# Attention on one Trainium2 core: the norm of the queries by products in four 32-column tiles beside the products with v, turned once, and one out-projection moved to the last tile

## The chip, the cores and the metric

The kernel runs on one core of a Trainium2 chip. The metric is the time on the device, in microseconds, of one execution of the whole program. The time before is the median of three runs; a separate execution was recorded by the hardware profiler, and every number on a stage or an instruction comes from that one.

## The reference

The program is a network of four layers on a sequence of 1024 tokens with 16 meta tokens ahead of them (1040 columns in the kernel, 9 blocks: one of 16 and eight of 128). Layers 0 and 3 are sliding-window attention, layer 1 an mLSTM, layer 2 an HGRN2. The change touches the attention layers alone.

```python
def rmsnorm(x, g):
    xf = x.astype(jnp.float32)
    y = xf * lax.rsqrt(jnp.mean(xf * xf, axis=-1, keepdims=True) + EPS)
    return (y * g.astype(jnp.float32)).astype(x.dtype)

def sliding_window_attention(q, k, v, sinks, valid):
    ...
    s = jnp.einsum('bnqhgd,bnkhd->bnhgqk', qb, kk) * (A_HD ** -0.5)
    ...
    s = jnp.where(mask[None, :, None, None], s, -jnp.inf)
    sink = sinks.astype(jnp.float32).reshape(A_KV, g, 1)
    m = jnp.maximum(s.max(axis=-1), sink)
    e = jnp.exp(s - m[..., None])
    p = e / (e.sum(axis=-1) + jnp.exp(sink - m))[..., None]
    o = jnp.einsum('bnhgqk,bnkhd->bnqhgd', p, vv)
    return o.reshape(bsz, lp, A_W)

def attention_branch(u, w_in, q_gain, k_gain, sinks, w_out, valid, pos):
    bsz, lp, _ = u.shape
    q, k, v, z = _split(u @ w_in, (A_W, A_KVW, A_KVW, A_W))
    q = rope(rmsnorm(q.reshape(bsz, lp, A_HEADS, A_HD), q_gain), pos)
    k = rope(rmsnorm(k.reshape(bsz, lp, A_KV, A_HD), k_gain), pos)
    v = v.reshape(bsz, lp, A_KV, A_HD)
    o = sliding_window_attention(q, k, v, sinks, valid)
    return (o * jax.nn.silu(z.astype(jnp.float32))).astype(u.dtype) @ w_out
```

There are 16 query heads and 4 key heads of 64 columns. The norm of q is one number for each token and head: the mean of 64 squares, to the power -1/2.

## The kernel before

**Layout.** Activations lie transposed: features on the 128 partitions, tokens along the free axis. The tokens are cut into three chunks, `CHUNKS`, of 400, 384 and 256 columns, with blocks (0, 1, 2, 3), (4, 5, 6) and (7, 8). In the last attention layer (layer 3) the 16 meta tokens are not needed as queries, so its chunks (`LAST_CHUNKS`) hold three, three and two blocks. One attention layer has eight tiles t = 0..7, each of 128 features: two query heads, hh = 0 and 1.

**Products.** Matmuls of a projection (`proj`, L255) run in a rounded type, as three products for high and low halves of weights and activations; weights come by DMA, and `split` (L188 on ScalarE, L189 on VectorE) makes the halves. Matmuls in plain f32 (the norm, the products with v) appear in the trace as two records each.

**Queries.** `qk_proj` projects one tile of q, chunk by chunk. `evac` (L520, L521) writes the scaled q and its squares, `sq`, into temporaries of the pool `t` (five buffers, three for each chunk), and issues four DMAs on SP that rotate q for rope. `finish` hangs three steps behind a chunk, at delays `D_Q` of 2000, 4000 and 6000 ns of planned work: the norm, rope, and `q_split`. For q the norm is `columns`: for each block one matmul with the squares of 128 tokens as weights and two columns of a mask as the moving operand (L535), which gives one column per head and a row per token; ScalarE takes the logarithm (L537) and two exponentials (L539) into the small tile `rs` (four buffers), and in chunk 0 GpSimd negates four of them (L541). `stat` (L546) is the norm of the keys and is not touched.

**Softmax.** `mixers` cuts a tile into pairs of units (blocks 0; 1; 2 and 3; 4 and 5; 6; 7 and 8, both heads). `S_step` makes the scores (L615, L616) and the softmax, which reads `rs`: copy (L635), select (L636), maximum (L637, L638), exponential (L640), reciprocal (L642) and scaling (L644). `T_step` turns the probabilities on TensorE (L661) and masks them into `Pt` (L664). `V_step` multiplies with v (L683), each head in 64 columns of the array, and on a unit marked last copies the result to the row `R["o", t]` (L686). In the list of steps V_step of pair k - 2 comes first, then for each head T_step of pair k - 1 and S_step of pair k.

**Order.** The order of TensorE is written out by hand, as a list of steps `[cost, function, prefetch]`; the other engines are put in order by the framework's scheduler, with the softmax steps at a higher priority. `weave` mixes the softmax steps of a tile with its fill, in proportion to planned cost. `chain` strings the fill together from `parts` and inserts the hanging steps at their due times; what is due after the end hangs over to the next tile (`hang`). The fill of tile t is the q projection of t + 1, the gate projection `zc[t - 1]` (from t = 1 on), in t = 0 of layer 3 the v projection, in t = 3 the second tile of keys, and an out-projection (`proj_out`, L338, with adds into x, L341) in t = 2 (`oc[1]`) and t = 4 (`oc[3]`). `oc[5]` and `oc[7]` follow after the layer. The splits of an out-projection's operand, `splits`, are put 2500 ns (`Y_AHEAD`) ahead of its products. The last loop of `layer_a` moves a `q_split` that would come too early behind the last scores of the tile before. The final loop of the program runs the list and issues each prefetch 12 us of planned work ahead.

**Buffers.** [...] The rows of o, k, cos and sin share nine buffers of the pool `r`.

Of the kernel before, what the change touches and what calls it, by code (L numbers as in the profile page):

```python
# [11 lines left out]
AF = mybir.ActivationFunctionType  # L12
ALU = mybir.AluOpType
PSUM = bass.MemoryType.PSUM

P = 128
# [13 lines left out]
def blk(b):  # L30
    return (0, NMETA) if b == 0 else (NMETA + P * (b - 1), P)
# [9 lines left out]
ROWS, TMPS, RAWS, YS, QS = 9, 5, 2, 3, 6  # L41
XS = 14
GAP, BURST = 200.0, 1300.0
KT_LAG = 500.0
NORM_AT = (4000.0, 0.7), (5000.0, 0.5), (8000.0, 0.5)
Y_LAST, Y_EARLY, Y_AHEAD = 3, 8, 2500.0
# [5 lines left out]
MM = 1.0 / 2.4  # L52
# [58 lines left out]
def hybrid_kernel(ctx: ExitStack, tc: tile.TileContext, ins, out, layers=(0, 1, 2, 3)):  # L111
# [38 lines left out]
    def psa():  # L150
        return psum("pa", 1)
# [289 lines left out]
    def layer_a(i, j, first, last, fin):  # L441
# [13 lines left out]
            sp.dma_start(R["cos"], ins["rope"][0])  # L455
            sp.dma_start(R["sin"], ins["rope"][1])

        order = {}

        def k_split(j):  # L460

# [53 lines left out]
        def qk_proj(src, gcol, work, fsplit, ch, scales=None):  # L515
            late = {}

            def evac(acc, n, c0, cn):
                late[n] = dst, sq, rot = work(n, c0, cn)
                s.activation(dst, acc[:, :cn], AF.Identity, scale=R["cons"][:, gcol : gcol + 1])  # L520
                s.activation(sq, acc[:, :cn], AF.Square)  # L521
                for q in range(4):
                    o = q ^ 1
                    sp.dma_start(rot[32 * q : 32 * q + 32], dst[32 * o : 32 * o + 32])

            def finish(n, c0, cn):
                cs = slice(c0, c0 + cn)

                def columns():
                    sq = late[n][1]  # L530
                    st, qcols = psa(), [blk(b)[0] - c0 for b in CHUNK_BLOCKS[n] if blk(b)[0] >= c0]
                    w = 2 * len(qcols)
                    R["rs", scales, n] = rs = small(24).rearrange("p (z b) -> p z b", z=3)
                    for k, z in enumerate(qcols):
                        pe.matmul(st[:, 2 * k : 2 * k + 2], sq[:, z : z + P], R["masks"][:, 0:P:64],  # L535
                                  start=True, stop=True)
                    s.activation(rs[:, 2, :w], st[:, :w], AF.Ln, bias=eps, scale=1.0 / 64)  # L537
                    for z, power in ((0, -0.5), (1, 0.5)):
                        s.activation(rs[:, z, :w], rs[:, 2, :w], AF.Exp, scale=power)  # L539
                    if n == 0:  # L540
                        g.tensor_scalar(rs[:, 2, :4], rs[:, 0, :4], -1.0, None, op0=ALU.mult)  # L541

                def stat():
                    dst, sq, rot = late[n]
                    st = psa()
                    pe.matmul(st[:, :cn], R["masks"][:, 0:P], sq, start=True, stop=True)  # L546
                    rstd_from(st, sq, cn, 64)

                def rope():
                    dst, sq, rot = late[n]  # L550
                    v.tensor_tensor(dst, dst, R["cos"][:, cs], op=ALU.mult)
                    v.tensor_tensor(rot, rot, R["sin"][:, cs], op=ALU.mult)
                    v.tensor_tensor(dst, dst, rot, op=ALU.add)
                    if scales is None:
                        v.tensor_tensor(dst, dst, sq, op=ALU.mult)

                first = [4 * cn * MM, stat, None] if scales is None else [110 * len(CHUNK_BLOCKS[n]), columns, None]
                return [(D_Q[0], first), (D_Q[1], [0.0, rope, None]),
                        (D_Q[2], fsplit(lambda: late[n][0], n, c0, cn))]

            return proj(src, evac, ch), [finish(n, *c) for n, c in enumerate(ch)]

# [36 lines left out]
        def mixers():  # L599
# [97 lines left out]
            for k in range(len(pairs) + 2):  # L697
                seg = pairs[k][0]["t"] if k < len(pairs) else 8
                v2, t1, s0 = (pairs[j] if 0 <= j < len(pairs) else None for j in (k - 2, k - 1, k))
                if v2:  # L700
                    put(seg, 470, V_step, v2, len(v2[0]["unit"]))
                for hh in range(2):
                    if t1:
                        put(seg, 110, T_step, t1[hh], len(t1[hh]["unit"]))
                    if s0:
                        step = put(seg, 236, S_step, s0[hh], len(s0[hh]["unit"]))
                        if s0[hh]["last"]:
                            order["S", s0[hh]["t"], s0[hh]["n"]] = step
            return segs

        zc = {t: gate_proj(win[12 + t], lambda t=t: R["o", t], chunks) for t in range(8)}
# [24 lines left out]
        for t in range(8):  # L736
# [7 lines left out]
            if t in (2, 4):  # L744
                z, (q, fin) = zc[t - 1], qg[t + 1]
                parts += [(flat(z[:2]), []), tile_of(q[:1], fin[:1]), (z[2], []), tile_of(q[1:], fin[1:])]
                splits, products = outs(oc[t - 1])
                parts.append((products, [(-Y_AHEAD, z) for z in splits]))
            elif t < 7:
                parts.append(tile_of(*qg[t + 1]))  # L750
            if t % 2 or t == 6:
                parts.append((flat(zc[t - 1]), []))
            fill, hang = chain(parts)
# [2 lines left out]
        for t in range(1, 8):  # L756
            for n in range(3):
# [2 lines left out]
                k = at.index(id(order["S", t - 1, n]))  # L760
                if q < k:
                    body.insert(k, body.pop(q))
        return head, body, oc[5], oc[7]

    def layer_b(i, j, fin):
# [708 lines left out]
```

## Time and profile before

| | us |
|---|---|
| median of three runs | 2649.59 |
| lowest and highest run | 2643.7 and 2650.41 |
| the profiled execution | 2639.39 |
| its span, first to last instruction | 2637.2 |
| mean granted TensorE clock in it | 0.997 |

The page of a profile gives for each engine its busy time; PE is TensorE's matmuls and PEld its weight loads, which run beside them. A row of a group of instructions names the line, the engine, the operation and the tiles (out<-in), then the shapes, the count, the busy time and the mean duration of one in ns, the idle time of the engine ahead of them and what ended it. A row of the timeline has the start and the length in us and the count of merged instructions. A row of busy times by stretch has the stretch, its length, then for PE, PEld, DVE, ACT and POOL the busy time and the count, the granted clock, the DMA share and GB/s.

In layer 0 the products with v (L683) lie between 77 and 435 us of the span, in layer 3 between 2236 and 2583 us; the two layers between are not touched.

### The profile page before, as it was taken

Reading aid. Unit: us, or ns where it says so; the run is one execution under the profiler, and the core shown is the slowest. Engines: PE = TensorE matmul, PEld = TensorE weight load, DVE = VectorE, ACT = ScalarE, POOL = GpSimd, SP = SyncE. Lnnn points to the kernel's source line nnn. Section 1 sums busy time; section 2 is a strip of 40 time slices with the busy share of each in tenths; the row PEclk is TensorE's granted clock in tenths of the full one; section 3 lists DMA queues with packets and bytes.
Section 4 is the critical chain, followed back from the end, with each engine's and each line's share of the span. In section 5 each row is a group of like instructions: output and inputs, shape, how many; then the busy total and the mean of one; then the engine's idle time right before and its main releaser. Section 6 shows DMA issues by size and latency. Waiting matters only on the chain.

```text
span 2637.2 us, 54958 instructions
## 1 busy us (share of the span) xinstructions
PE 2578.4 (98%) x20848; PEld 2460.5 (93%) x20848; DVE 1880.7 (71%) x5127; ACT 1672.0 (63%) x4525; POOL 147.9 (6%) x465
## 2 busy tenths in 40 slices
PE   7999999999999999999999999999999999999999
PEld 6899988899999999999999999999999999999989
DVE  6777777974747474647464678979787979677776
ACT  7768686565454545454544657878585867768683
POOL 1000000000000000000000000111001001000000
PEclk9999999999999999999999999999999999999999
DMA  4211111021111111111111101011110111111102
GB/s 139 60 36 49 52 38 39 25 66 57 41 49 43 55 41 57 41 57 41 57 41 49 48 27 50 26 38 34 38 38 30 42 62 45 53 45 52 50 25 88
DMA packets 74040, 126.80 MB, mean 48 GB/s; under 512 B 11552, under 2 KB 25760, under 8 KB 73776
## 3 DMA queue, kind: packets, MB, share of 16 engines
q1 hardware_dynamic: 73776, 123.29, 15.0%
q8 instruction: 164, 2.69, 0.4%
q14 instruction: 100, 0.82, 0.1%
HBM read 108.40 MB, written 4.26 MB: 43 GB/s over the span
## 4 chain that ended last, share of the span: by engine, by line
PE 77%; DVE 12%; ACT 7%; issue 2%; DMA 2%; SPq 0%; POOL 0%; DVEq 0%; ACTq 0%; POOLq 0%
PE pj L255 36%; PE pj L338 16%; PE pj L300 10%; PE po L683 2%; PE po L898 1%; PE pa L912 1%; PE pt L661 1%; DVE t L408 1%; PE po L900 1%; PE pm L615 1%; DVE ul L189 1%; PE pm L616 1%; PE pa L535 1%; ACT Sm L640 1%; DVE X L1117 1%
## 5 line engine op out<-in xcount | busy, mean ns | idle before, releaser
L255 PE MATMUL pj<-uh,wh 128*128 128x384 f32 (+2 forms) x2592 | 889.2, 343 | 3.1 <-ACT uh L188 3.1
L255 PE MATMUL pj<-ul,wh 128*128 128x384 f32 (+2 forms) x2592 | 834.4, 322 | 2.9 <-DVE ul L189 2.7
L255 PE MATMUL pj<-uh,wl 128*128 128x384 f32 (+2 forms) x2592 | 832.2, 321 | 0.1
L255 PEld LDWEIGHTS pj<-uh,wh 128*128 128x128 f32 x2592 | 490.5, 189 | 32.1 <-issue 17.0
L255 PEld LDWEIGHTS pj<-ul,wh 128*128 128x128 f32 x2592 | 490.5, 189 | 12.6 <-DVE ul L189 5.5
L255 PEld LDWEIGHTS pj<-uh,wl 128*128 128x128 f32 x2592 | 490.1, 189 | 0.5 <-DVE wl L189 0.4
L189 DVE TENSOR_TENSOR wl<-wr,wh 128x512 fp32r<-128x512 f32 x336 | 228.5, 687 | 55.4 <-ACT wh L188 52.1
L300 PE MATMUL pj<-wh,uh 128*128 128x256 f32 x896 | 267.6, 299 | 0.0
L341 DVE TENSOR_TENSOR x<-x,pj 128x384 f32<-128x384 f32 (+2 forms) x480 | 234.8, 509 | 40.4 <-PE pj L338 38.6
L188 ACT CAST wh<-wr 128x512 fp32r<-128x512 f32 x337 | 202.8, 615 | 90.7 <-PE pj L338 28.4
L338 PE MATMUL pj<-yh,wh 128*128 128x384 f32 (+2 forms) x768 | 252.2, 328 | 0.0
L300 PE MATMUL pj<-wh,ul 128*128 128x256 f32 x896 | 251.9, 281 | 0.0
L300 PE MATMUL pj<-wl,uh 128*128 128x256 f32 x896 | 251.8, 281 | 0.0
L338 PE MATMUL pj<-yl,wh 128*128 128x384 f32 (+2 forms) x768 | 247.4, 322 | 3.1 <-DVE yl L189 3.1
L338 PE MATMUL pj<-yh,wl 128*128 128x384 f32 (+2 forms) x768 | 247.0, 322 | 0.0
L300 PEld LDWEIGHTS pj<-wh,uh 128*128 128x128 f32 x896 | 168.7, 188 | 2.6 <-issue 0.3
L300 PEld LDWEIGHTS pj<-wl,uh 128*128 128x128 f32 x896 | 168.8, 188 | 2.0
L300 PEld LDWEIGHTS pj<-wh,ul 128*128 128x128 f32 x896 | 168.8, 188 | 0.0
L428 DVE SCALAR_TENSOR_TENSOR t<-pj,t 128x384 f32<-128x384 f32 (+2 forms) x192 | 98.6, 514 | 98.1 <-ACT t L427 97.7
L429 ACT ACTIVATE t<-t 128x384 f32<-128x384 f32 (+2 forms) x240 | 117.7, 490 | 77.8 <-DVE t L428 76.7
L188 ACT CAST yh<-r 128x384 fp32r<-128x384 f32 (+2 forms) x120 | 57.4, 478 | 154.4 <-PE pj L338 139.9
L338 PEld LDWEIGHTS pj<-yl,wh 128*128 128x128 f32 x768 | 144.9, 189 | 5.0 <-DVE yl L189 4.7
(236 smaller groups left out, 5129.0 us busy)
## 6 DMA issues: line engine op xcount, KB each, us to landing
wr<-in_b_win SPq DMA_DIRECT2D x128, 256.0 KB, 2.8
wr<-in_a_win SPq DMA_DIRECT2D x80, 256.0 KB, 2.7
wr<-in_c_win SPq DMA_DIRECT2D x64, 256.0 KB, 2.7
r<-rowsd SPq DMA_DIRECT2D x16, 520.0 KB, 5.4
wr<-in_a_wout SPq DMA_DIRECT2D x32, 256.0 KB, 2.8
wr<-in_b_wout SPq DMA_DIRECT2D x32, 256.0 KB, 2.7
t<-t SPq DMA_DIRECT2D x96, 48.0 KB, 2.0
wr<-in_c_wout SPq DMA_DIRECT2D x16, 256.0 KB, 2.7
```

The source lines that it names most:

```text
L188: s.copy(h, src)
L189: v.tensor_tensor(l, src, h.bitcast(F32), op=ALU.subtract)
L255: pe.matmul(acc[:, :cn], a[:, k, :], b[:, k, c0 : c0 + cn], start=(k == 0 and i == 0), stop=(k == KT - 1 and i == 2))
L300: pe.matmul(acc[:cn, :256], a[:, k, c0 : c0 + cn], m[:, kk, :], start=(k == 0 and i == 0), stop=(k == KT - 1 and i == 2))
L338: pe.matmul(acc[:, :cn], a[:, k, mc], b, start=(k == 0 and i == 0), stop=(k == 1 and i == 2))
L341: v.tensor_tensor(x[:, m, c0 : c0 + cn], x[:, m, c0 : c0 + cn], acc[:, :cn], op=ALU.add)
L408: v.scalar_tensor_tensor(u, x[:, k, cs], ngain[:, self.i, k : k + 1], self.acc[n], op0=ALU.mult, op1=ALU.mult)
L428: v.scalar_tensor_tensor(a[:, :cn], z, 0.0, a[:, :cn], op0=ALU.min, op1=ALU.subtract)
L429: s.activation(a[:, :cn], a[:, :cn], AF.Exp)
L535: pe.matmul(st[:, 2 * k : 2 * k + 2], sq[:, z : z + P], R["masks"][:, 0:P:64], start=True, stop=True)
L615: pe.matmul(S[:nq, u, :kw], q[:, qb], kh[:, kb], start=True, stop=False)
L683: pe.matmul(po[64 * hh : 64 * hh + 64, q0 - c0 : q0 - c0 + nq], V[kb][:kn, vc : vc + 64], ws[hh]["Pt"][:kn, u, ki, :nq], start=(ki == 0), ...
```

## The change

The norm of q in `finish` becomes two steps. `columns` now uses 32 columns of the mask as weights (16 that pick head 0 and 16 that pick head 1) and streams the squares of a block, 128 tokens, so that block k lands on partitions 32k to 32k + 31 of one PSUM bank; the logarithm of these rows, 128 wide, goes back into `sq`. Before, the result had a token on each partition; now it has the heads there and the tokens along the free axis. `turned`, a new step, transposes the used rows (32 for each block) on TensorE with the identity, and takes the two exponentials from every 16th column of the result into `rs`. In chunk 0 GpSimd now negates two columns.

`turned` is due `TURN_LAG`, 1500 ns of planned work, after `columns`. A new loop at the end of `layer_a` then takes each pair of steps: it looks for the next V_step (`bursts`) behind `columns`, puts `columns` directly behind it and `turned` at least 1500 ns of planned work later, if both still come ahead of the first scores that need them (`order["S0", ...]`); else both stay. The norm of tile 0 lies partly in the head of the layer, which the loop doesn't see.

The out-projection `oc[3]` leaves the fill of t = 4 and becomes the first part of t = 7, ahead of `zc[6]`; its first two splits stand directly before its products.

```diff
--- before.py
+++ after.py
@@ -41,6 +41,7 @@
 ROWS, TMPS, RAWS, YS, QS = 9, 5, 2, 3, 6
 XS = 14
 GAP, BURST = 200.0, 1300.0
+TURN_LAG = 1500.0
 KT_LAG = 500.0
 NORM_AT = (4000.0, 0.7), (5000.0, 0.5), (8000.0, 0.5)
 Y_LAST, Y_EARLY, Y_AHEAD = 3, 8, 2500.0
@@ -455,7 +456,7 @@
             sp.dma_start(R["cos"], ins["rope"][0])
             sp.dma_start(R["sin"], ins["rope"][1])
 
-        order = {}
+        order, bursts = {}, set()
 
         def k_split(j):
 
@@ -526,19 +527,27 @@
             def finish(n, c0, cn):
                 cs = slice(c0, c0 + cn)
 
+                qcols = [blk(b)[0] - c0 for b in CHUNK_BLOCKS[n] if blk(b)[0] >= c0]
+                rows = 32 * len(qcols)
+
                 def columns():
                     sq = late[n][1]
-                    st, qcols = psa(), [blk(b)[0] - c0 for b in CHUNK_BLOCKS[n] if blk(b)[0] >= c0]
-                    w = 2 * len(qcols)
-                    R["rs", scales, n] = rs = small(24).rearrange("p (z b) -> p z b", z=3)
+                    st = psa()
                     for k, z in enumerate(qcols):
-                        pe.matmul(st[:, 2 * k : 2 * k + 2], sq[:, z : z + P], R["masks"][:, 0:P:64],
+                        pe.matmul(st[32 * k : 32 * k + 32, :P], R["masks"][:, 48:80], sq[:, z : z + P],
                                   start=True, stop=True)
-                    s.activation(rs[:, 2, :w], st[:, :w], AF.Ln, bias=eps, scale=1.0 / 64)
+                    s.activation(sq[:rows, :P], st[:rows, :P], AF.Ln, bias=eps[:rows], scale=1.0 / 64)
+
+                def turned():
+                    pt = psum("pt", 1)
+                    pe.transpose(pt[:, :rows], late[n][1][:rows, :P], ident[:rows, :rows])
+                    pv = pt[:, :rows].rearrange("p (b h c) -> p b h c", h=2, c=16)[:, :, :, 0]
+                    R["rs", scales, n] = rs = small(24).rearrange("p (z b h) -> p z b h", z=3, h=2)
                     for z, power in ((0, -0.5), (1, 0.5)):
-                        s.activation(rs[:, z, :w], rs[:, 2, :w], AF.Exp, scale=power)
+                        s.activation(rs[:, z, : len(qcols)], pv, AF.Exp, scale=power)
                     if n == 0:
-                        g.tensor_scalar(rs[:, 2, :4], rs[:, 0, :4], -1.0, None, op0=ALU.mult)
+                        g.tensor_scalar(rs[:, 2, :2], rs[:, 0, :2], -1.0, None, op0=ALU.mult)
+                    R["rs", scales, n] = rs.rearrange("p z b h -> p z (b h)")
 
                 def stat():
                     dst, sq, rot = late[n]
@@ -554,9 +563,12 @@
                     if scales is None:
                         v.tensor_tensor(dst, dst, sq, op=ALU.mult)
 
-                first = [4 * cn * MM, stat, None] if scales is None else [110 * len(CHUNK_BLOCKS[n]), columns, None]
-                return [(D_Q[0], first), (D_Q[1], [0.0, rope, None]),
-                        (D_Q[2], fsplit(lambda: late[n][0], n, c0, cn))]
+                rest = [(D_Q[1], [0.0, rope, None]), (D_Q[2], fsplit(lambda: late[n][0], n, c0, cn))]
+                if scales is None:
+                    return [(D_Q[0], [4 * cn * MM, stat, None])] + rest
+                order["st", scales, n] = a = [230, columns, None]
+                order["tu", scales, n] = b = [110, turned, None]
+                return [(D_Q[0], a), (D_Q[0] + TURN_LAG, b)] + rest
 
             return proj(src, evac, ch), [finish(n, *c) for n, c in enumerate(ch)]
 
@@ -698,7 +710,7 @@
                 seg = pairs[k][0]["t"] if k < len(pairs) else 8
                 v2, t1, s0 = (pairs[j] if 0 <= j < len(pairs) else None for j in (k - 2, k - 1, k))
                 if v2:
-                    put(seg, 470, V_step, v2, len(v2[0]["unit"]))
+                    bursts.add(id(put(seg, 470, V_step, v2, len(v2[0]["unit"]))))
                 for hh in range(2):
                     if t1:
                         put(seg, 110, T_step, t1[hh], len(t1[hh]["unit"]))
@@ -706,6 +718,8 @@
                         step = put(seg, 236, S_step, s0[hh], len(s0[hh]["unit"]))
                         if s0[hh]["last"]:
                             order["S", s0[hh]["t"], s0[hh]["n"]] = step
+                        if s0[hh]["first"] and hh == 0:
+                            order["S0", s0[hh]["t"], s0[hh]["n"]] = step
             return segs
 
         zc = {t: gate_proj(win[12 + t], lambda t=t: R["o", t], chunks) for t in range(8)}
@@ -744,10 +758,14 @@
             if t in (2, 4):
                 z, (q, fin) = zc[t - 1], qg[t + 1]
                 parts += [(flat(z[:2]), []), tile_of(q[:1], fin[:1]), (z[2], []), tile_of(q[1:], fin[1:])]
-                splits, products = outs(oc[t - 1])
-                parts.append((products, [(-Y_AHEAD, z) for z in splits]))
+                if t == 2:
+                    splits, products = outs(oc[1])
+                    parts.append((products, [(-Y_AHEAD, z) for z in splits]))
             elif t < 7:
                 parts.append(tile_of(*qg[t + 1]))
+            if t == 7:
+                splits, products = outs(oc[3])
+                parts.append((splits + products, []))
             if t % 2 or t == 6:
                 parts.append((flat(zc[t - 1]), []))
             fill, hang = chain(parts)
@@ -760,6 +778,23 @@
                 k = at.index(id(order["S", t - 1, n]))
                 if q < k:
                     body.insert(k, body.pop(q))
+        for t in range(8):
+            for n in range(3):
+                at = [id(z) for z in body]
+                a, b = (at.index(id(order[z, t, n])) if id(order[z, t, n]) in at else -1 for z in ("st", "tu"))
+                if a < 0:
+                    continue
+                k = next((k for k in range(a, len(body)) if at[k] in bursts), -1)
+                end, lag = k + 1, 0.0
+                while k > 0 and end < len(body) and lag < TURN_LAG:
+                    lag += body[end][0]
+                    end += 1
+                if k > 0 and max(end, b) < at.index(id(order["S0", t, n])):
+                    later_turn = max(end, b + 1)
+                    body.insert(later_turn, body[b])
+                    body.insert(k + 1, body[a])
+                    del body[b + (b > k)]
+                    del body[a]
         return head, body, oc[5], oc[7]
 
     def layer_b(i, j, fin):
```

## The prediction

> **What bounds the kernel now.** I read the page first (span, engines, chain), then the busy time of each engine by stage, then the timeline of TensorE at the places that the diff touches.
>
> ```profile
> span 2637.2 us, 54958 instructions
> PE 2578.4 (98%) x20848; PEld 2460.5 (93%) x20848; DVE 1880.7 (71%) x5127; ACT 1672.0 (63%) x4525; POOL 147.9 (6%) x465
> PE 77%; DVE 12%; ACT 7%; issue 2%; DMA 2%; SPq 0%; POOL 0%; DVEq 0%; ACTq 0%; POOLq 0%
> ```
>
> TensorE is the bound: 98% busy and 77% of the chain that ended last. So only two things count: TensorE time that the products themselves take, and the holes where TensorE stands still. A busy PE hides small holes, since the ends of matmuls overlap; the weight loader (PEld) shows them better, because in a dense stretch it is never idle.
>
> The stages below are the tiles t of an attention layer, cut at the first score product of each t. The first four rows are t = 4, 5, 6, 7 of layer 0, the next four the same of layer 3. After the time and the length come PE, PEld, DVE, ACT and POOL, then the clock.
>
> ```profile
> 259.10:318.00 58.90, 58.90 (x426) 55.89 (x424) 45.88 (x123) 38.23 (x118) 3.56 (x13) 1.00 0.15 41
> 318.00:357.00 39.00, 38.45 (x289) 34.30 (x287) 27.83 (x81) 29.43 (x98) 3.67 (x13) 1.00 0.16 49
> 357.00:394.90 37.90, 37.14 (x281) 33.08 (x280) 28.31 (x83) 30.02 (x100) 3.49 (x12) 1.00 0.15 43
> 394.90:426.70 31.80, 25.98 (x190) 21.74 (x190) 21.25 (x69) 24.62 (x79) 3.03 (x10) 0.95 0.06 19
> ...
> 2421.20:2476.90 55.70, 55.70 (x407) 53.47 (x406) 43.15 (x113) 36.15 (x111) 2.69 (x10) 1.00 0.16 44
> 2476.90:2512.90 36.00, 35.60 (x277) 33.04 (x276) 26.48 (x73) 27.43 (x90) 3.31 (x11) 1.00 0.17 52
> 2512.90:2549.10 36.20, 35.28 (x271) 31.83 (x270) 28.06 (x78) 29.93 (x97) 3.31 (x11) 1.00 0.15 45
> 2549.10:2575.95 26.85, 24.71 (x187) 20.91 (x188) 19.56 (x60) 22.52 (x74) 2.38 (x8) 1.00 0.06 18
> ```
>
> Subtract PEld from the length: in layer 0 the loader idles 3.01, 4.70, 4.82 and 10.06 us in t = 4 to 7, in layer 3 it idles 2.23, 2.96, 4.37 and 5.94. The stage with an out-projection (t = 4) has the fewest holes, the last tile by far the most: there only one gate projection lies beside the softmax. What TensorE waits for there, in layer 0:
>
> ```profile
> PEld pt L661 <- ACT Sm L644: 7.0, 8, 2.0
> PE pt L661 <- ACT Sm L644: 5.5, 4, 1.8
> ...
> 397.40:400.00 2.60, 2.60 (x12) 2.38 (x13) 1.38 (x5) 1.43 (x5) 0.18 (x1) 0.50 0.00 0
> ```
>
> The turn of the probabilities (L661) waits for their scaling (L644), the end of a chain through ACT and DVE. After holes of up to 2.0 us the granted clock was 0.50 in these 2.60 us, which costs 1.3 us more.
>
> **The out-projection that moves.** oc[3] (48 products for each of three column chunks; x144 records a layer) leaves t = 4 and stands at the head of t = 7, before zc[6]. Nothing of it is added or dropped, so its price is what its cover is worth. I take for t = 7 the holes of today's t = 4: layer 0 gains 10.06 - 3.01 = 7.05, plus 1.3 for the clock, 8.3 us; layer 3 gains 5.94 - 2.23 = 3.7 us. In t = 4 the cover is gone, and what is late next is the same turn L661; the stage then looks like t = 5 and 6 (mean 4.76 in layer 0, 3.67 in layer 3), so it loses 1.8 and 1.4 us. Net 6.5 + 2.3 = 8.8 us.
>
> ```profile
> L338 PE MATMUL pj<-yl,wh 128*128 128x384 f32 (+2 forms) x768 | 247.4, 322 | 3.1 <-DVE yl L189 3.1
> ```
>
> The splits of y stood 2.5 us of planned work ahead and now stand directly before their product. Over all 768 records these waits come to 3.1 us today, so I take nothing here and bound it by 1.5 us a layer. Four weight loads move with the step; SP has no rotation of q to issue in t = 7 and the DMA share there is 0.06. DVE gets its adds into x and the weight splits: t = 4 spends 45.88 - 27.83 = 18.1 us more on it than t = 5, and TensorE's loader 21.6 more. So t = 7 would be some 21.7 + 21.6 + 3.0 = 46 us long with DVE busy 39 of it, 85%, where t = 4 has 78%. For that I leave 0.5 us of holes a layer: **7.8 us gained** by the move. As lower end I take twice the loss in t = 4 (3.2 us less) and late splits (3 us less): 1.8 us.
>
> **The norm products that are replaced.**
>
> ```profile
> 63.76 0.34 PE L255 MATMUL pj<-uh,wl 128*128 128x384 f32 x1
> 63.93 0.95 PE L535 MATMUL pa<-masks,t 128*128 128x2 f32 x8
> 64.74 0.42 PE L255 MATMUL pj<-uh,wh 128*128 128x384 f32 x1
> 65.00 0.34 PE L255 MATMUL pj<-ul,wh 128*128 128x384 f32 x1
> 65.17 0.34 PE L255 MATMUL pj<-uh,wl 128*128 128x384 f32 x1
> ...
> L535 PE MATMUL pa<-masks,t x272: 165/251/272, 63.9 to 2534.2; 128*128 128x2 f32 x136
> L537 ACT ACTIVATE s<-pa,eps x48: 244/264/273, 66.0 to 2542.7; 128x6 f32<-128x6 f32 x24, 128x4 f32<-128x4 f32 x16, 128x8 f32<-128x8 f32 x8
> ```
>
> Each product is two records. From 63.76 to 65.00 lie two products of L255 at a pitch of 0.175 (65.00 to 65.17 and 63.76 to 63.93) and the eight records: 1.24 - 0.35 = 0.89 us, 0.111 a record. The 48 groups (8 of four blocks, 24 of three, 16 of two) cost 272 x 0.111 = 30.2 us.
>
> What they become is bounded by products in column tiles:
>
> ```profile
> 203.26 0.28 PE L338 MATMUL pj<-yh,wl 128*128 128x256 f32 x1
> 203.47 0.66 PE L683 MATMUL po<-Pt,v 128*64 128x128 f32 x8
> 204.06 0.45 PE L255 MATMUL pj<-uh,wh 128*128 128x400 f32 x1
> 204.35 0.34 PE L255 MATMUL pj<-ul,wh 128*128 128x400 f32 x1
> 204.53 0.34 PE L255 MATMUL pj<-uh,wl 128*128 128x400 f32 x1
> ...
> 110.00 1.09 PE L683 MATMUL po<-Pt,v 128*64 128x128 f32 x16
> ...
> 1696.82 0.37 PE L1143 MATMUL pm<-X 128*32 128x32 f32 x23
> ...
> L1143 PE MATMUL pm<-X 128*32 128x32 f32 (+1 forms) x2624 | 34.2, 199 | 2.5 <-DVE X L1120 2.4
> ```
>
> Sixteen records of L683 span 1.09 us, eight 0.66: 0.43 for eight more, which run two abreast, 0.108 a pair. Going into column tiles and back costs the rest: 203.26 to 204.35 is 1.09, less 0.12 (L338) and 0.18 (L255) is 0.79, less 0.43 is 0.36 us. L1143 has the form of the new product (128 rows, 32 columns): 23 records span 0.37 us and one lasts 0.199, so they start 8 ns apart, where a pass over 32 columns takes 0.108 / 4 = 27 ns: more than three abreast. With 128 columns streamed, two passes of four tiles take 2 x 0.108 = 0.22 us, for two blocks as for four.
>
> Behind a product with v the array is already in column tiles, but of 64 columns, and no row shows a step from 64 to 32. Bounds: 0 and the full 0.36; I take 0.15, the way in (203.26 to 203.47 is 0.09 over the pitch; the rest is the first weights, loaded with no cover). So 0.37 us beside V_step. Six groups (tile 0 of both layers, whose norm lies ahead of any V_step) stay alone at 0.22 + 0.36 = 0.58.
>
> [...]
>
> The turn is one transpose more in each group:
>
> ```profile
> 200.21 0.28 PE L338 MATMUL pj<-yh,wl 128*128 128x256 f32 x1
> 200.32 0.27 PE L661 MATMUL pt<-const,Sm 128*128 128x128 f32 x1
> 200.35 0.36 PE L338 MATMUL pj<-yh,wh 128*128 128x256 f32 x1
> 200.56 0.28 PE L338 MATMUL pj<-yl,wh 128*128 128x256 f32 x1
> ...
> 1701.44 0.46 PE L1215 MATMUL pa<-v,kT 16*128 16x128 f32 x2
> 1701.83 0.70 PE L1234 MATMUL pa<-t,const 128*128 128x256 f32 x2
> ```
>
> From 200.21 to 200.56 are two products of 0.12 and one turn: 0.12 us; 48 make 5.8. The 16 turns of two blocks have 64 rows. The nearest row has 16 rows, and its two records take 0.39 instead of 0.22; I take 0.2 more for each, 3.2 us, with 0 as the other end. Sum after: 42 x 0.37 + 6 x 0.58 + 5.8 + 3.2 = 28.0, against 30.2: **2.2 us gained**; with no switch cost at all 18.5 (11.7 gained), with 0.36 everywhere 36.8 (6.6 lost).
>
> **The new wait.** The turn reads what Ln wrote, so TensorE, which runs in order, now waits for ACT; behind it stand the scores and turns of the softmax and the projections. The planner leaves 1.5 us or a step more. Today:
>
> ```profile
> 82.98 0.61 PE L535 MATMUL pa<-masks,t 128*128 128x2 f32 x4
> 83.63 0.26 ACT L537 ACTIVATE s<-pa,eps 128x4 f32<-128x4 f32 x1
> ...
> 101.54 0.72 PE L535 MATMUL pa<-masks,t 128*128 128x2 f32 x6
> 104.67 0.27 ACT L537 ACTIVATE s<-pa,eps 128x6 f32<-128x6 f32 x1
> ```
>
> The first, right behind a product with v, has its Ln done 0.3 us after the group's end; the second 2.7 us after, 0.2 to 1.2 beyond the gap. Bounds: 0, and 48 x 0.5 = 24 us. The first place is the one to which the change moves the groups, so I take 1 us. Ln grows from 4 to 8 columns to 128 on ACT; if that doubled its 0.264 us, 48 of them would be 13 us, which I price at nothing because ACT is idle a fifth of these stages. The Pool step shrinks and is off the path.
>
> **Sum.** -7.8 - 2.2 + 1 = **-9.0 us**. The profiled execution took 2639.39 us (span 2637.2 and 2.2 around it), 10.2 below the median of the runs, 2649.59; on its scale the forecast is 2630.4, on that of the medians **2640.6**.
>
> **Rivals.**
> - *No switch between 64 and 32 columns.* 6.3 us less, and 3.2 less if 64-row turns are free: -15 to -19, 2633. For it: both are column modes over 128 rows. Against: no row shows it.
> - *The holes go to t = 4.* If t = 4 pays twice what t = 5 and 6 show and the splits are late, 3.2 + 3 us come off: about -3, 2647. For it: ACT is busy 38.23 us in today's t = 4, 8.8 more than in t = 5, and only the casts of weights and y leave with the move. Against: t = 5 and 6 have the same fill.
> - *The groups do not come beside V_step* (the planner refuses the place): all 48 at 0.58, +6.6 instead of -2.2: 0, 2649. *Or the four tiles run one after another*: 136 x 0.22 in place of 48 x 0.22 is 19 us more: +10, 2660. L1143 speaks against it.
> - *The turns wait.* Slower than before if the mean wait of 48 turns is above 0.21 us (10.0 us of gains in 48), and by more than 0.3% above 0.37; at 0.6 us +19, 2668. For it: the row of 101.54. Against: that of 82.98.
>
> **Chances.** Forecast 0.44, no switch 0.25, t = 4 pays 0.16, not beside 0.05, one after another 0.03, turns wait 0.07. About 0.3%, 7.9 us, is what a measurement of this kernel can tell from no change. The forecast's own spread, -5 to -14, puts a quarter of itself within that (0.11): faster 0.25 + 0.33 and 0.01 of t = 4's, 0.59; same 0.11 + 0.15 + 0.05 = 0.31; slower 0.10. The range goes from 2626 (no switch at all and no waits) to 2652 (unchanged, with the runs' own scatter), leaving out the turns that wait, the serial tiles and a tail below.
>
> **What would show it.** In the profile after: PEld idle in t = 7 of about 3 us (layer 0) and clock 1.00 there; t = 4 some 38 us long with idle near 5; groups of the new product of some 0.4 us behind L683; few waits of the turn for Ln. I am wrong if the turn stands high among the waits of PE, if TensorE waits in t = 7 for the splits, or if a buffer kept longer (sq until the turn, the rows of o for tiles 2 and 3 until t = 7) holds up ACT.

## The result, and the profile after

The change took the median of fourteen runs from 2648.34 us (2640.24 to 2654.53) to 2639.77 (2636.13 to 2642.61): a ratio of 0.9973, with a 95% interval from 0.9962 to 0.9983, or 7.1 us (4.5 to 10.1) less. A ratio, here and below, is not the quotient of the two medians beside it; these lie 8.6 us apart. The forecast was 2640.6 us and 9.0 us less. One execution of e2 below, 2796.82 us at a granted clock of 0.849, was in a slower state; its median counts it, its ratio does not.

The profiled executions say the opposite, 2639.39 us before and 2641.85 after: the one of before lies below all fourteen runs. And 4.0 us of the difference lie in layers 1 and 2, which the change does not touch. From the first transpose of the gates in layer 1 to the last one of the keys in layer 2 pass 1600.0 us before and 1604.0 after, and 1599.9 and 1604.5 in a second profile of each. The 130 records of TensorE at its start take 14.30 us at a clock of 1.00 before and 15.80 at 0.89 after. Why this comes with the change is open. So gains below are read from ratios of runs, and only places and causes from the traces.

The page after, its span and engines.

```profile
span 2639.8 us, 55105 instructions
PE 2578.2 (98%) x20896; PEld 2445.3 (93%) x20896; DVE 1878.5 (71%) x5127; ACT 1675.0 (63%) x4525; POOL 148.4 (6%) x465
```

TensorE is still the bound. The weight loader is busy 15.2 us less (2460.5 to 2445.3): 272 wide weight loads, 35.1 us, became 272 narrow ones and 48 turns, 14.4 us together. This alone says nothing of holes: the loads of L537 take 7.7 us beside 18.5 of its products, so the loader also idles where TensorE works. The waits below show the holes.

The busy time of each engine by stage, after: t = 4 and 7 of layer 0, then of layer 3, cut at the first score product of each t, with the columns of the table before.

```profile
260.54:297.84 37.30, 37.09 (x286) 32.63 (x284) 27.90 (x84) 30.23 (x98) 3.76 (x13) 1.00 0.12 37
...
376.68:418.06 41.38, 41.38 (x303) 38.45 (x301) 32.03 (x89) 25.40 (x77) 2.82 (x9) 1.00 0.12 39
2423.86:2461.52 37.66, 35.39 (x275) 31.82 (x274) 27.95 (x79) 32.17 (x102) 3.64 (x11) 1.00 0.14 41
...
2535.46:2575.41 39.95, 39.92 (x293) 37.65 (x293) 30.97 (x85) 25.06 (x71) 2.43 (x8) 1.00 0.12 41
```

Length less PEld: in t = 7 the loader now idles 2.93 and 2.30 us at a clock of 1.00. Before it idled 10.06 and 5.94, or 9.39 and 5.63 where the stage is cut, as here, at its last score product. In t = 4 it idles 4.67 and 5.84 (before 3.01 and 2.23). That is the move, as forecast.

The groups by line: busy us, mean ns, idle time ahead and what ended it. The turn of the probabilities before (L661):

```profile
L661 PE MATMUL pt<-const,Sm 128*128 128x128 f32 x224 | 52.4, 288 | 15.5 <-ACT Sm L644 15.4
```

After: the products of the new norm, its turn, and the turn of the probabilities, now L673.

```profile
L537 PE MATMUL pa<-t,masks 128*32 128x128 f32 x272 | 18.5, 283 | 0.0
L543 PE MATMUL pt<-const,t 96*128 96x96 f32 (+2 forms) x48 | 13.1, 282 | 9.7 <-ACT t L539 9.7
L673 PE MATMUL pt<-const,Sm 128*128 128x128 f32 x224 | 51.4, 285 | 7.5 <-ACT Sm L656 7.4
```

Two rows of the list of waits after (total us, times, longest):

```profile
PE pt L543 <- ACT t L539: 9.7, 10, 4.3
PE pj L339 <- DVE yl L190: 3.1, 6, 0.7
```

The turn of the probabilities waits 7.5 us where it waited 15.5, and beside it the new turn of the norm (L543) stands 9.7 us for the logarithm (L539): ten waits, one of 4.3 us. The late splits of y (L190) cost 3.1 us, as before the change.

That longest wait, in the timeline of TensorE at the head of layer 3:

```profile
2223.72 0.42 PE L537 MATMUL pa<-t,masks 128*32 128x128 f32 x6
2228.44 0.42 PE L543 MATMUL pt<-const,t 96*128 96x96 f32 x1 [4.30 <-ACT t L539]
2228.57 0.56 PE L627 MATMUL pm<-r,qs 128*128 128x256 f32 x1
```

And ScalarE in the same stretch:

```profile
2223.83 0.47 ACT L521 ACTIVATE t<-pj,cons 128x256 f32<-128x256 f32 x1 [0.77 <-PE pj L256]
2224.45 0.51 ACT L474 CAST r<-r 64x384 fp32r<-64x384 f32 x1
...
2227.08 0.38 ACT L522 ACTIVATE t<-pj 128x256 f32<-128x256 f32 x1
2227.49 0.51 ACT L477 CAST kl<-kl 64x384 fp32r<-64x384 f32 x1
2228.03 0.36 ACT L539 ACTIVATE t<-pa,eps 96x128 f32<-96x128 f32 x1
```

The turn was due 1500 ns of planned work behind its products and stands directly behind them. In the head of the layer the function `spread` lays hanging steps among the products of one chunk and puts whatever is due after the chunk's end at that end. The planner believes in 1.5 us of distance; there is none. On ScalarE the logarithm stands behind seven instructions from 2224.45 on, six casts of the keys (L474 to L477) and one scaling of q (L522), and TensorE, in order, behind the logarithm. The clock then drops, as the busy times of two stretches show (before and after the turn):

```profile
2223.70:2228.40 4.70, 0.44 (x7) 0.15 (x6) 4.22 (x10) 4.29 (x10) 0.00 (x0) 0.98 0.46 146
2228.40:2231.60 3.20, 3.16 (x15) 3.16 (x16) 2.59 (x6) 2.69 (x8) 0.00 (x0) 0.50 0.08 21
```

By an estimate from its 0.50 over 3.20 us this costs another 1.6: the products of L297 start every 0.21 us in that stretch, and every 0.12 from 2231.68 on. The theory to test: the move is worth more than forecast, the norm by itself makes the kernel slower through this wait. The rivals: the norm gains as forecast and the move less; or the groups beside the products with v cost more than they save.

### The profile page after: what moved, and what is told of

Read it like the earlier page. It is cut to its first block, busy times and chain, and to the rows that moved or that the text cites. A ratio compares the mean times of both kernels' runs of the same rounds, so it can differ in the third digit from the quotient of the medians.

```text
span 2639.8 us, 55105 instructions
## 1 busy us (share of the span) xinstructions
PE 2578.2 (98%) x20896; PEld 2445.3 (93%) x20896; DVE 1878.5 (71%) x5127; ACT 1675.0 (63%) x4525; POOL 148.4 (6%) x465
## 4 chain that ended last, share of the span: by engine, by line
PE 76%; DVE 12%; ACT 8%; issue 2%; DMA 2%; SPq 0%; POOL 0%; DVEq 0%; ACTq 0%; POOLq 0%
PE pj L256 35%; PE pj L339 16%; PE pj L301 10%; PE po L695 2%; PE po L933 1%; ACT Sm L652 1%; DVE t L409 1%; PE pa L947 1%; PE pt L673 1%; PE po L935 1%; DVE ul L190 1%; PE pm L627 1%; PE pm L628 1%; PE pj L297 1%; DVE X L1153 1%
## 5 line engine op out<-in xcount | busy, mean ns | idle before, releaser
L190 DVE TENSOR_TENSOR wl<-wr,wh 128x512 fp32r<-128x512 f32 x336 | 228.3, 687 | 56.8 <-ACT wh L189 53.9
```

What stands on the lines that cost most here:

```text
L190: v.tensor_tensor(l, src, h.bitcast(F32), op=ALU.subtract)
```

## The experiments

All ratios are to the kernel before, timed beside each one.

| | edit | median us | ratio and 95% interval |
|---|---|---|---|
| e1_move_only | before with the move alone | 2636.67 | 0.9964 (0.9952 to 0.9976) |
| e2_norm_only | after without the move | 2655.59 | 1.0020 (1.0007 to 1.0033) |
| e3_late_turn | after, one turn later | 2636.59 | 0.9952 (0.9937 to 0.9966) |
| e4_full_turn | after, turns of 128 rows | 2635.55 | 0.9952 (0.9934 to 0.9969) |
| e5_before_again | before, unchanged | 2646.06 | 0.9999 (0.9986 to 1.0012) |
| e6_late_full | both edits of e3 and e4 | 2627.80 | 0.9926 (0.9910 to 0.9943) |
| e7_not_beside | e6, no group moved beside V_step | 2640.90 | 0.9971 (0.9959 to 0.9982) |
| e8_lag_3000 | e6, twice the lag | 2631.43 | 0.9940 (0.9925 to 0.9954) |
| e9_norm_mended | e6 without the move | 2643.64 | 0.9990 (0.9979 to 1.0002) |
| e10_after_again | after, unchanged | 2639.79 | 0.9981 (0.9970 to 0.9991) |

**The two parts apart.** In e1 the kernel before gets the out-projection in t = 7 and nothing else; in e2 the kernel after has it back in t = 4.

```diff
-                splits, products = outs(oc[t - 1])
-                parts.append((products, [(-Y_AHEAD, z) for z in splits]))
+                if t == 2:
+                    splits, products = outs(oc[1])
+                    parts.append((products, [(-Y_AHEAD, z) for z in splits]))
...
+            if t == 7:
+                splits, products = outs(oc[3])
+                parts.append((splits + products, []))
```

> The kernel before with the out-projection oc[3] in t = 7 and nothing else changed. Theory A (the move fills the holes of the last tile, and the new norm gives with one hand and takes with the other): 8 to 14 us faster than before; PEld idle in t = 7 of layer 0 near 3 us, of layer 3 near 2 us. Theory B (the gain of the change is the shorter norm products, and the holes only wander to t = 4): within 4 us of before.

> The changed kernel with oc[3] back in t = 4: the new norm alone. Theory A: products and turns 3.3 us shorter (272 records at 0.111 us against 42 groups at 0.36, six at 0.54, 32 turns at 0.12 and 16 at 0.31), waits of the turn for Ln of 9.7 us and some clock lost behind the longest, so 4 to 9 us slower than before. Theory B: 5 us or more faster than before.

The move alone gains 0.36%, 9.5 us (6.4 to 12.7). The norm alone loses 0.20%, 5.3 us (1.9 to 8.7). Added, that is 4.2 us gained, just outside the interval of the whole change (4.5 to 10.1) but with an uncertainty of over 4 us of its own. The stages t = 4 and 7 of e1, layer 0 and then layer 3:

```profile
261.02:299.88 38.86, 38.25 (x283) 34.77 (x282) 27.59 (x84) 30.46 (x98) 4.05 (x13) 0.97 0.13 38
379.82:422.65 42.83, 41.61 (x302) 38.44 (x301) 32.30 (x91) 26.06 (x80) 3.22 (x9) 1.00 0.11 38
2418.83:2454.70 35.87, 35.05 (x273) 32.66 (x272) 27.94 (x79) 30.43 (x97) 3.61 (x11) 1.00 0.14 41
2528.08:2567.91 39.83, 39.83 (x292) 37.62 (x292) 30.96 (x84) 24.92 (x72) 2.31 (x8) 1.00 0.13 41
```

The loader idles 4.09 and 3.21 us in t = 4, 4.39 and 2.21 in t = 7: the holes of t = 7 fill up and t = 4 opens by about 1 us a layer, without the new norm having any part in it. In layer 0 the stage ahead of it, t = 3, opens as well: its loader idles 6.03 us, where it idled 4.84. The turn of the probabilities, by line, in e1 and then in e2:

```profile
L661 PE MATMUL pt<-const,Sm 128*128 128x128 f32 x224 | 50.9, 285 | 11.3 <-ACT Sm L644 11.1
```

```profile
L673 PE MATMUL pt<-const,Sm 128*128 128x128 f32 x224 | 52.2, 288 | 11.7 <-ACT Sm L656 11.6
```

From 15.5 us of waiting the move alone takes 4.2 and the norm alone 3.8, and 15.5 less both is 7.5, as in the kernel after. So a part of what TensorE waits for the new turn it no longer waits for the softmax. That the softmax gets on while TensorE stands at the turn is the likely reason; e8 below shows the same trade in the other direction.

**Two mends of the norm.** In e3 only the turn of the second chunk of tile 0, which falls at the end of the head in layer 3, is taken out of the head and hung 3 us into the tiles.

```diff
-                grp += spread(groups[n], ev[i])
+                grp += spread(groups[n], [e for e in ev[i] if e[1] is not order.get(("tu", 0, 1))])
...
-        hang = ev[0] + ev[1]
+        hang = ev[0] + ev[1] + [(3000.0, order["tu", 0, 1])]
```

> The changed kernel with one turn put later: that of tile 0, chunk 1 in layer 3, which the head flushes directly behind its products, is due 3 us into the fill of tile 0. Theory A (that wait of 4.30 us, with the clock at half for some 2.4 us after it, is the largest single loss of the change): 4 to 6 us faster than the changed kernel, so 12 to 15 us faster than before, and no wait of L543 above 1.5 us. Rival (ScalarE's work of the key splits is what the start of tile 0 waits for, whoever stands first in TensorE's queue): within 1.5 us of the changed kernel, with the wait found at another line.

In e4 every turn transposes 128 rows; the rows that are not logarithms are squares, and no exponential reads what becomes of them.

```diff
-                    pe.transpose(pt[:, :rows], late[n][1][:rows, :P], ident[:rows, :rows])
+                    pe.transpose(pt[:, :P], late[n][1][:, :P], ident)
```

> The changed kernel with every turn on all 128 rows; the rows beyond those of the blocks are squares that nobody reads. If a turn of 64 rows pays for going into and out of a half-height array (0.31 us against 0.12 in the trace), the 16 turns of two blocks lose 0.19 us each: 3 us faster than the changed kernel, and the start after the turn follows by 0.03 us and not by 0.20. If not: within 1 us, and the 0.20 us stay.

The waits of the turn for the logarithm (total us, times, longest), in e3 and in e4:

```profile
PE pt L543 <- ACT t L539: 5.4, 9, 1.3
```

```profile
PE pt L543 <- ACT t L539: 8.6, 9, 4.0
```

In e3 the wait of 4.3 us is gone, and its time with it: 0.21% better than after, 5.6 us, where 4.3 and the 1.6 estimated for the slow clock make 5.9. The two intervals leave an uncertainty of about 5, but the place itself agrees: from these products of the norm to the fifth score product behind them (L627) pass 14.27 us after and 9.22 in e3, 5.0 less. So ScalarE's splits of the keys did not hold up the scores themselves, and that rival falls. In e4 the wait is still there; what goes is the turn of 64 rows. TensorE in the kernel after, at such a turn:

```profile
2285.86 0.34 PE L256 MATMUL pj<-uh,wl 128*128 128x384 f32 x1
2286.13 0.27 PE L543 MATMUL pt<-const,t 64*128 64x64 f32 x1
2286.33 0.44 PE L669 MATMUL pt<-const,Sm 128*128 128x128 f32 x2
```

The same place in e4:

```profile
2284.03 0.34 PE L256 MATMUL pj<-ul,wh 128*128 128x384 f32 x1
2284.21 0.34 PE L256 MATMUL pj<-uh,wl 128*128 128x384 f32 x1
2284.39 0.27 PE L543 MATMUL pt<-const,t 128*128 128x128 f32 x1
2284.49 0.38 PE L669 MATMUL pt<-const,Sm 128*128 128x128 f32 x2
```

The start of the turn comes 0.27 us after the product ahead of it with 64 rows and 0.18, the product's own pitch, with 128; the next product comes 0.20 and 0.10 later (0.03 was expected). So half the rows cost 0.19 us more, not less: 16 times 0.19 is 3.0 us. The runs give 0.21%, 5.6 us, with an uncertainty of about 5 by the two intervals; whether the mend is worth more than 3 is not settled.

**Both mends, and what the place is worth.**

> The changed kernel with both mends: the late turn in the head of layer 3, and every turn on 128 rows. If the two losses are what the traces show (4.3 us of wait and the clock behind it; 16 x 0.19 us), they add: 7 to 9 us faster than the changed kernel, 14 to 17 us faster than before. If they are one effect of the schedule: about 5 us faster than the changed kernel.

In e7 the loop that looks for a V_step moves nothing, so it doesn't hold the turn 1.5 us of planned work behind its products either. In e8 the turn comes at least 3000 ns of planned work after the logarithm's products.

```diff
-                if k > 0 and max(end, b) < at.index(id(order["S0", t, n])):
+                if False and max(end, b) < at.index(id(order["S0", t, n])):
```

```diff
-TURN_LAG = 1500.0
+TURN_LAG = 3000.0
```

> e6_late_full with the norm products left where they are due, not put behind a product with v. If entering the column tiles is what counts, 42 groups pay 0.54 us and not 0.36: 7 us slower than e6_late_full. Rival (the place behind a product with v costs as much as it saves, by the wait for Ln and by the time that the squares are kept): within 2 us.

> e6_late_full with the turn due 3000 ns of planned work after its products in place of 1500. If the waits for Ln that are left (nine of 0.4 to 1.4 us, 6 to 7 us in all) are real losses: 3 to 6 us faster than e6_late_full, and L543 waits under 1.5 us in all. If ScalarE's work is late in any case, the wait moves to the scores or the next turn of probabilities: within 2 us.

The engines on the page of e6, then on that of e7:

```profile
PE 2576.6 (98%) x20896; PEld 2448.3 (93%) x20896; DVE 1878.0 (71%) x5127; ACT 1675.5 (64%) x4525; POOL 147.7 (6%) x465
```

```profile
PE 2583.2 (98%) x20896; PEld 2448.1 (93%) x20896; DVE 1880.6 (71%) x5127; ACT 1677.6 (64%) x4525; POOL 147.8 (6%) x465
```

The waits of the turn in e6, then in e7:

```profile
PE pt L543 <- ACT t L539: 4.6, 8, 1.0
```

```profile
PE pt L543 <- ACT t L539: 9.2, 11, 2.3
```

e6 is the fastest kernel of the study, 0.74% (0.57 to 0.90) below the one before: 19.6 us (15 to 24) where 14 to 17 were expected, and 12 us, with an uncertainty of about 5, below the changed kernel where 7 to 9 were. So the two losses add; whether e6 gains more than both is not settled.

e7 is 0.45% worse than e6, 12 us with an uncertainty of about 5, where 7 were expected from groups at 0.54 us and not at 0.36. The rows show two parts: TensorE is busy 6.6 us longer (2583.2 - 2576.6), and waits 4.6 us longer (9.2 - 4.6) for the logarithm. The first fits what a group costs by its place: read from start to start, one alone among full-width products costs 0.54 us (in the kernel after 65.03 to 65.93, less two products of 0.18), and one behind 16 records of a product with v only adds 0.35 (1.13 us to the next dense product without it, 1.48 with it). The second belongs to the place and to the distance together, as e7 gives up both; that ScalarE's queue is shorter behind a product with v is not shown apart. The rival of groups that cost more there than they save falls.

e6 has eight such waits, 4.6 us, where the expectation counted on nine and 6 to 7 us. In e8 they all but vanish, and the time does not follow: 0.9940 against 0.9926, with intervals that overlap. Its waits of the turn:

```profile
PE pt L543 <- ACT t L539: 1.5, 2, 0.8
```

Its turn of the probabilities, and its group of the exponentials behind the turn (L547):

```profile
L673 PE MATMUL pt<-const,Sm 128*128 128x128 f32 x224 | 51.5, 285 | 8.9 <-ACT Sm L656 8.5
L547 ACT ACTIVATE s<-pt 128x6 f32<-128x6 f32 (+2 forms) x96 | 11.3, 175 | 5.1 <-PE pt L543 4.9
```

TensorE waits 3.1 us less at the turn of the norm and 2.8 more at that of the probabilities (8.9, where e6 has 6.1, in the row shown further below), and ScalarE now stands 4.9 us for the turns. So the second expectation came true: the wait has moved, and the waits that are left are not worth mending by a longer lag.

**The mended norm alone.** e9 is e6 with the out-projection back in t = 4, by the edit of e2.

> e6_late_full with oc[3] back in t = 4: the mended norm without the move. If the two parts add (the move alone 0.36%, both together 0.74%): 8 to 12 us faster than before. By the count of TensorE's time alone (products and turns 6.3 us shorter than the old ones, 6.7 us of waits left): within 3 us of before; what is more must then come from holes that the new order closes and from the clock behind them.

The norm no longer loses: -0.10%, 2.6 us less (5.6 less to 0.5 more). That is what the count of TensorE's time gave, within 3 us, and not the 8 to 12 of parts that add. With e1's 0.36% that makes 0.46, and both together give 0.74. The gap of 0.28 has an uncertainty of about 0.24, so that the two parts help one another is likely and not settled. One place differs most: t = 3 of layer 3 lasts 53.1 us in e9 and 48.7 in e6. Not all of that is lost time: the stage holds 13 more records, the turn waits 1.92 us there and not 0.98, and the clock is 0.97 and not 1.00.

**The same kernels again.**

> The kernel before, unchanged, for a second profile: its first one took 2639.4 us where the median of its runs is 2648. Theory A (the runs differ by TensorE's granted clock behind the holes of the attention layers): a slower execution shows its extra time in the heads of layers 0 and 3 and in the tiles, with a lower clock there. Rival (it is in the two layers that the change does not touch): the extra time is in layers 1 and 2.

> The changed kernel, unchanged, for a second profile. If the clock behind holes is what makes runs of one kernel differ, the loader's idle time in each stage is the same as in its first profile within 0.2 us, and the lengths differ by up to 3 us where the clock does. The waits of L543 stay at 9 to 10 us with one of 4.3 in the head of layer 3.

Neither has moved: 0.9999 and 0.9981 (0.9970 to 0.9991), beside 0.9973 for the first timing of the change. The second profile of the change has the same waits of the turn (9.7 us in ten, one of 4.3), and in all sixteen stages the loader idles as long as in the first, within 0.2 us. What the second profile of before shows is the last section.

## Why the prediction was right, and where it was wrong

The time was right, 2640.6 against 2639.77, and so was the sign. But it came out of a sum in which one cost was put at a tenth of what it is and the gains were too cautious, and these errors cancel: that the number came out so near is in part luck. By the prediction's own mark, that 0.3% is what a measurement can tell from no change, the 0.27% lies just below it.

- **The bound.** Right: TensorE before and after, and most of what was gained and lost was found where its loader stood still. In a dense stretch of the kernel before, from 200.00 to 203.00, the loader is busy 3.00 of 3.00 us.
- **The move, "7.8 us gained".** Right in mechanism, and measured alone at 9.5 (6.4 to 12.7). Holes of t = 7: 2.93 and 2.30 us for a forecast of 3.01 and 2.23. Holes of t = 4: the forecast was today's 3.01 + 1.8 and 2.23 + 1.4, and e1 has 4.09 and 3.21; in the kernel after, layer 3 has 5.84, as a wait of the new turn falls there. The 1 us taken off for a busy VectorE was not due: it is busy 32.03 of 41.38 us in t = 7, 77%, not 39 of 46. In layer 0 the stage gained 124 records up to its last scores (179 to 303), not the 144 of the projection: 129 of these are done by then, and the rest follows behind, so it is shorter than the 46 us forecast. One slip of the prediction changes nothing: 7.8 less 3.2 and 3 is 1.6, not the 1.8 given as lower end.
- **The splits, taken at nothing.** Right: the same 3.1 us as before.
- **The norm products, "2.2 us gained".** Right in mechanism, and less than half of what they save. A group beside a product with v, and a place with two groups, in the timeline of the kernel after:

```profile
97.00 1.09 PE L695 MATMUL po<-Pt,v 128*64 128x128 f32 x16
98.03 0.43 PE L537 MATMUL pa<-t,masks 128*32 128x128 f32 x8
98.39 0.39 PE L256 MATMUL pj<-uh,wh 128*128 128x256 f32 x1
...
130.15 0.63 PE L537 MATMUL pa<-t,masks 128*32 128x128 f32 x10
130.71 0.45 PE L256 MATMUL pj<-uh,wh 128*128 128x400 f32 x1
```

  From its start to the product behind it are 0.36 us, where 0.37 was forecast, whatever a step from 64 to 32 columns costs included. No run shows the 0.15 us that the forecast holds for that step by itself; the runs show the 0.36 as a whole. But two groups at one place take 0.56, not 0.72, and eight places have two; 28 have one, and only four groups stand alone, at 0.54. A turn of 64 rows costs 0.09 + 0.20 = 0.29 (forecast 0.32). With 28 x 0.36, 8 x 0.56, 4 x 0.54, the forecast's 32 x 0.12 and 16 x 0.29 the new norm takes 25.2 us, 5.0 less than the old 30.2. The rival without a switch, by which a group beside V_step takes 0.22, falls.
- **The new wait, "I take 1 us".** This is the step that failed: it measured 9.7 us, with an estimated 1.6 more of slow clock behind the longest. The prediction's own sign of being wrong came true, as the turn now stands highest among TensorE's waits. The prediction bounded it from 0 to 24 and chose the low end by one row, in which the logarithm follows a product with v. The norm's products stand in 40 places, and 36 of them are right behind a product with v, so the place was as forecast and the wait was not. Nearly half of the wait is one place that never sees a product with v, the end of layer 3's head, where ScalarE had seven other instructions first. The mean over 48 turns, 0.20 us, stands just below 0.21, from which the rival of the waiting turns makes the kernel slower; with the estimated 1.6 us of slow clock it is 0.24.
- **What the prediction left out.** It priced a wait of the turn in full. But e2 shows 3.8 us less of waiting at the turn of the probabilities. For the norm alone: 5.0 - 9.3 (the wait in e2) - 1.6 + 3.8 = -2.1, so 2.1 us worse, where e2 measured 5.3 (1.9 to 8.7); so by itself the norm is what the rival of the waiting turns said, slower than before.
- **The sum.** 9.5 + 5.0 - 9.7 - 1.6 + 3.8 = 7.0 us gained by the measured terms and the estimated 1.6, and 7.1 (4.5 to 10.1) by the runs. For e6 it is 9.5 + 5.0 + 3.0 - 4.6 and, from the group of its turn below, 15.5 - 6.1 - 4.2 = 5.2: 18.1, where the runs give 0.74%, 19.6 us (15 to 24).

```profile
L673 PE MATMUL pt<-const,Sm 128*128 128x128 f32 x224 | 50.7, 283 | 6.1 <-ACT Sm L656 6.0
```

  Both sums lie inside their intervals. They hold no term for the 4 us in layers 1 and 2, nor for the clock at other places, so an agreement closer than some 3 us means nothing.
- **Buffers kept longer.** This shows, but is small. ScalarE, writing temporaries of the gate projection (L426), now stands for the turn, which frees `sq`; before, it had no such wait:

```profile
ACT t L426 <- PE pt L543: 1.6, 4, 0.6
```

## What to carry to other kernels

Before work that ends in a transpose is handed to TensorE, ask what stands ahead of the step between on the other engine's queue, at each place and not at a typical one: TensorE takes its list in order (in the 4.30 us ahead of the turn at 2228.44 none of the products behind it started), so one place in the head of a layer, with 4.3 us and a slow clock, cost more (5.9, of which 1.6 are estimated) than all the new products saved (5.0). A due time in a planner is a wish; look up where the step lands when its group ends sooner. And measure the parts of a change apart, since here one part was hiding the loss of another, and two small mends gained by the ratios more than the change itself (12 us and 7).

## What the runs showed that was not expected

**The same hole, another clock.** Two profiled executions of the kernel before, the unchanged program, differ by 4.8 us (2639.39 and 2644.16), and not in their holes. Layers 1 and 2 take 1600.0 and 1599.9 us, so the rival that looked for the time there falls. Of the sixteen stages of layers 0 and 3 three differ by more than 0.1 us in length, all in layer 0 and all at a lower clock in the slower execution: t = 0, 1 and 7 (0.95, 0.96 and 0.84). At the start of t = 1 of layer 0, the 2 us of a hole and then 2 us that begin 4 us after its start; first the profile shown above as that of before:

```profile
105.80:107.80 2.00, 0.24 (x4) 0.09 (x1) 1.79 (x7) 1.97 (x9) 0.00 (x0) 1.00 0.20 50
109.80:111.80 2.00, 2.00 (x24) 1.73 (x22) 1.76 (x7) 1.30 (x5) 0.00 (x0) 1.00 0.03 8
...
105.84:147.65 41.81, 39.58 (x298) 35.70 (x297) 30.55 (x89) 32.70 (x110) 3.67 (x13) 1.00 0.13 36
394.94:425.22 30.28, 24.58 (x179) 20.89 (x180) 19.73 (x63) 23.25 (x76) 3.03 (x10) 0.94 0.06 18
```

Then the second profile of the same kernel, at the same work:

```profile
107.30:109.30 2.00, 0.25 (x4) 0.10 (x1) 1.78 (x7) 1.97 (x9) 0.00 (x0) 1.00 0.20 50
111.30:113.30 2.00, 2.00 (x20) 1.73 (x18) 1.69 (x7) 0.69 (x3) 0.00 (x0) 0.51 0.00 0
...
107.34:150.67 43.33, 41.10 (x297) 37.03 (x296) 30.57 (x89) 32.76 (x110) 3.70 (x13) 0.96 0.12 34
397.88:430.59 32.71, 27.38 (x179) 23.31 (x180) 19.73 (x63) 23.38 (x76) 2.77 (x10) 0.84 0.05 17
```

The holes are alike to 0.01 us, PE busy 0.24 and 0.25 of 2.00. Four us later the granted clock is 1.00 in the one and 0.51 in the other. The stage t = 1 lasts 41.81 and 43.33 us, t = 7 30.28 and 32.71, while the loader's idle time is the same within 0.2 us (6.11 and 6.30, 9.39 and 9.40). So behind two holes that are alike, 1.84 us of waiting (L661) in the first execution, the clock fell in one execution and not in the other; what decides it is not shown.

So the hole at the start of t = 1 costs its own length in both executions, and 1.5 us more in one of them. In t = 7, with several holes, the clock falls in both, to a mean of 0.94 and 0.84. In the kernel after, the hole at the start of t = 1 is nearly closed. The new norm at its new place does it: e1, without the new norm, still waits 1.86 us there, e2 as little as the kernel after (there 0.24 us for the logarithm and 0.37 for the scaling), and in e7, with the products elsewhere, the turn of the norm waits 2.01 us:

```profile
107.10:109.10 2.00, 1.63 (x10) 1.38 (x11) 1.48 (x5) 1.96 (x9) 0.18 (x1) 1.00 0.11 31
```

In t = 7 the move has closed most of them.

**The clock and the scatter of the runs.** Every execution has its mean granted clock on record. Of the 68 of the kernel before that were timed beside the experiments, 15 had 0.993 and took 2648.7 us in the mean, 14 had 0.995 and took 2644.3, three had 0.997 and took 2641.2. That is some 2 us for each 0.001, where 0.001 of 2640 us would be 2.6. So one kernel's runs differ by the clock in the main. At 0.995, 13 executions of the kernel after took 2640.5 us: 3.8 less than those of before. By this estimate about half of the 7.1 us is work and waiting saved, and the rest comes with a higher mean clock (0.9952 over 22 executions, 0.9940 over the 68).

Whether the change also narrows the scatter is not shown. In the first timing the runs of the kernel before lie over 14.3 us, those of the kernel after over 6.5; in e5 and e10, eight executions each, it is 7.9 and 8.2, and e1, which closes the holes of t = 7 too, lies over 13.4.
